# Gate of the latent attention: two heads with features on partitions, or four heads with tokens on partitions and transposes

## The chip, the cores and the metric

One core of a Trainium2 chip runs the whole program. The metric is the device time of one execution, in microseconds (us); the median of three runs of the kernel before is 2054.03 us.

The engines in this text are TensorE (PE in the profile, its weight loads are PEld), VectorE (DVE), ScalarE (ACT) and the queue that issues the loads from memory (SP). Each works through its own list of instructions in the order in which the list stands; semaphores make one engine wait for another.

## What is computed

Two layers of a network over 256 positions (tokens) of width 2048. Each layer normalises its input to `h`, multiplies it by one wide matrix `w_in`, and runs two branches; the change is in the second, the latent attention with 16 heads:

```python
proj = h @ w_in
rq, rk, rv, rg, cq, ckv, kr, mg, bg = jnp.split(proj, points, axis=-1)
q  = (rms_norm(cq, g_cq) @ w_uq)      # per head 128 + 64 (rotary) columns
kv = (rms_norm(ckv, g_ckv) @ w_ukv)   # per head 128 key and 128 value columns
o_mla = mla_attention(q_nope, q_rope, k_nope, k_rope, v)   # chunk-causal softmax
y_mla = (o_mla * jax.nn.silu(mg)) @ w_mla_proj
```

`mg` is the gate of the title: 2048 columns of `h @ w_in`, 128 for each head. All arithmetic is in fp32.

## The kernel before, in words

Matrix products run in three passes. A weight slice of 1024 values per partition is loaded into a tile `wst` (five buffers), ScalarE writes its high part into a tile `whl` (L240), VectorE the rest, the low part (L241), and TensorE multiplies high by high, high by low and low by high (L273 twice, L276 once, in `chunk`; `mm3` on L263 to L265 is the same for small operands). There are three `whl` buffers, so the split of a slice waits until the matmuls of the slice three before it are over.

`proj` gives a product with features on partitions: the weights are the stationary operand, `h` streams with 256 columns. `proj_tok` gives it with tokens on partitions: `h` is stationary, the weights stream with 512 columns, and two accumulators are filled, one for each half of the tokens. Accumulators `acc` come from four buffers in PSUM, other PSUM tiles `aux` from four more.

The attention loop (from `for g in range(MH // 2)`) does a pair of heads per turn, eight turns per layer. A turn has these steps: the query projection (36 matmuls from `cq`), whose results go to `qkn` and, through `rope_mla` (L483 to L485, VectorE), to the rotary part; the key and value projection (48 matmuls from `ckv`); the scores (L848, L849, `mm3`); the softmax (L852 to L866, on VectorE and ScalarE); the gate projection `mg` (L874, L875: 96 matmuls, then a Silu on ScalarE); the transposes of the softmax's result `sm` (L882), split into `p1` (L883) and copied to `pT` (L884); the product with the values (L888, L889) into `po`; the multiplication of `po` by the gate (L891, VectorE), and the split into `z` (L892), which `w_mla_proj` is multiplied with later.

A scheduler that knows the dependencies and the number of buffers orders each engine's list when the program is built. It mixes turns: the values product of a turn stands among the projections of the next. In the background, slices of `w_mod` for a later stage are loaded at a fixed rate per weight slice and accumulated on VectorE (L402, L367 when one is finished). Each weight slice's split has raised priority.

Of the kernel before, what the change touches and what calls it, by code (L numbers as in the profile page):

```python
# [13 lines left out]
AF = mybir.ActivationFunctionType  # L14
ALU = mybir.AluOpType
AX = mybir.AxisListType

P = 128
S = 256
# [19 lines left out]
C_MG = C_KR + ROPE  # L39
# [69 lines left out]
def trunk(ctx: ExitStack, tc: tile.TileContext, x, c, positions, w_mod, b_mod, g_norm, w_in, g_cq,  # L109
          g_ckv, w_uq, w_ukv, w_ret_proj, w_mla_proj, w_out, g_final, consts, decay, out):  # L110
    nc = tc.nc
    V, A, T, DMA = nc.vector, nc.scalar, nc.tensor, nc.sync
# [11 lines left out]
    def acc_tile():  # L124
        return pacc.tile([P, 2, S], F32, name="acc", tag="acc")

    def aux_tile():
        return paux.tile([P, 512], F32, name="aux", tag="aux")

    def tmp_tile():  # L130
        return tp.tile([P, 512], F32, name="tmp", tag="tmp")
# [4 lines left out]
    def quarter(name, dtype=F32):  # L136
        return big.tile([P, 1024], dtype, name=name, tag="quarter")
# [5 lines left out]
    def tokens(name):  # L143

        return quarter(name).rearrange("p (t f) -> p t f", t=2)
# [20 lines left out]
    ident = cst[:, K_ID : K_ID + P]  # L166
# [72 lines left out]
    def split_into(hi, lo, src):  # L239
        A.activation(hi, src, AF.Copy)  # L240
        return V.tensor_tensor(lo, src, hi.bitcast(F32), ALU.subtract)  # L241
# [7 lines left out]
    def load_split(src, nk, n, early=False):  # L249
        if prepared and not early:  # L250
            return prepared.pop(0)
        bg()
        w = load(src, nk, n)
        t = hp.tile([P, 2, 1024], F32R, name="whl", tag="whl")
        hi = t[:, 0, : nk * n].rearrange("p (k n) -> p k n", k=nk)
        lo = t[:, 1, : nk * n].rearrange("p (k n) -> p k n", k=nk)
        with tc.high_priority(offset=SPLITS):
            last_split.append(split_into(hi, lo, w))
        return hi, lo
# [7 lines left out]
    def chunk(todo):  # L267


        for o, w, a, start, _, moves in todo:  # L270
            for i in range(2):
                x, y = (a[i], w[0]) if moves else (w[0], a[i])
                T.matmul(o, x, y, start=start and i == 0, stop=False, skip_group_check=True)  # L273
        for o, w, a, _, stop, moves in todo:
            x, y = (a[0], w[1]) if moves else (w[1], a[0])
            T.matmul(o, x, y, start=False, stop=stop, skip_group_check=True)  # L276

    def proj_chunk(accs, hi, lo, k0, nk, span, act):

        chunk([(accs[j // 2][:, j % 2, :], (hi[:, k, j * P : (j + 1) * P], lo[:, k, j * P : (j + 1) * P]),  # L280
                act.block(k0 + k), k0 + k == span[0] and j % 2 == 0, k0 + k == span[1] - 1, False)
               for k in range(nk) for j in range(hi.shape[2] // P)])

    def proj(w, col, n, act, span=(0, KT)):
        accs = [acc_tile() for _ in range((n + 2 * P - 1) // (2 * P))]
        nk = 1024 // n
        for k0 in range(*span, nk):
            hi, lo = load_split(w[k0 * P : (k0 + nk) * P, col : col + n], nk, n)
            proj_chunk(accs, hi, lo, k0, nk, span, act)
        return accs  # L290

    def proj_tok(w, col, act, span=(0, KT)):

        accs = [acc_tile() for _ in range(2)]
        for k0 in range(*span, 2):
            hi, lo = load_split(w[k0 * P : (k0 + 2) * P, col : col + 512], 2, 512)
            chunk([(accs[t].rearrange("p a b -> p (a b)"), (hi[:, k, :], lo[:, k, :]),
                    act.block(k0 + k, slice(t * P, (t + 1) * P)), k0 + k == span[0], k0 + k == span[1] - 1, True)
                   for k in range(2) for t in range(2)])
        return [a.rearrange("p a b -> p (a b)") for a in accs]  # L300
# [325 lines left out]
    def layer(l, r, u):  # L626
        W = w_in[l]

        if l == 0:
            r, hh = start()  # L630
        else:
            hh = Pairs("h")
# [93 lines left out]
        for sg in range(2):  # L726
# [5 lines left out]
            for pr in range(2):  # L732
                g = 2 * sg + pr
# [6 lines left out]
                for h in range(2):  # L740
                    ps = aux_tile()
# [5 lines left out]
                    po = aux_tile()  # L747
# [42 lines left out]
        for g in range(MH // 2):  # L790
            def two(t, f0, n):
                return t[:, f0 : f0 + 2 * n].rearrange("p (a b) -> p a b", a=2)

            t1 = quarter("qkn")
            qn, kn, qr = two(t1, 0, P), two(t1, 256, P), t1[:, 512:768]
            t1 = quarter("q1", F32R)
            q1, r1 = (two(t1, 0, P), two(t1, 256, P)), (t1[:, 512:640], t1[:, 640:768])
            t1 = quarter("k1", F32R)
# [4 lines left out]
            for k0 in (0, 2):  # L803
                w = load(w_uq[l, k0 * P : (k0 + 2) * P, g * 2 * QW : (g + 1) * 2 * QW], 2, 2 * QW)
                w = w.rearrange("p k (h d) -> p k h d", h=2)
                t = hp.tile([P, 2, 1024], F32R, name="whl", tag="whl")
# [5 lines left out]
                for k in range(2):  # L812
                    kt = k0 + k
                    b = cq.block(kt)
# [10 lines left out]
            for k0 in (0, 2):  # L825
                hi, lo = load_split(w_ukv[l, k0 * P : (k0 + 2) * P, g * 512 : (g + 1) * 512], 2, 512)
                todo = []
                for k in range(2):
                    kt = k0 + k
                    b = ckv.block(kt)  # L830
# [15 lines left out]
            for h in range(2):  # L846
                ps = aux_tile()
# [17 lines left out]
                    i = 2 * t + h  # L865
                    V.tensor_scalar(sm[:, h, rng[t]], sm[:, h, rng[t]], rec[:, i : i + 1], None, ALU.mult)  # L866

            t1 = quarter("mg")
            mg, pT = two(t1, 0, S), two(t1, 512, P)
            t1 = quarter("p1", F32R)  # L870
            p1 = two(t1, 0, S), two(t1, 512, S)
            t1 = quarter("v1", F32R)
            v1 = t1[:, 0:256], t1[:, 256:512]
            accs = proj(W, C_MG + g * 256, 256, hh)  # L874
            A.activation(mg, accs[0], AF.Silu)  # L875

            split_into(*v1, vv[:, 0, :])
            po = aux_tile()
            for h in range(2):
                ps = aux_tile()  # L880
# [4 lines left out]
            for h in range(2):  # L885
# [1 line left out]
                o = po[:, h * S : (h + 1) * S]  # L887
                mm3(o, [u[:, es] for u in v1], [u[:, h, :] for u in p1], True, False)  # L888
                T.matmul(o[:, P:S], vv[:, 1, es], pT[:, h, :], start=False, stop=True, skip_group_check=True)  # L889
            zt = tmp_tile()  # L890
            V.tensor_tensor(zt, po, mg.rearrange("p a b -> p (a b)"), ALU.mult)  # L891
            split_into(*zz.flat(g), zt)  # L892


# [2 lines left out]
        for n in range(4):  # L897
# [6 lines left out]
            for a in range(2):  # L904
                ps = aux_tile()
                for b in range(2):
                    f = (2 * a + b) * P
# [9 lines left out]
        for f0, nf in ((0, 4), (4, 4), (8, 4), (12, 2), (14, 2)):  # L917
            accs = proj(w_out[l], f0 * P, nf * P, mm)
            with tc.high_priority() if f0 == 14 else nullcontext():
                for a, acc in enumerate(accs):  # L920
                    for b in range(2):
                        f = f0 + 2 * a + b
# [91 lines left out]
    for l in range(DEPTH):  # L1014
        r, u = layer(l, r, u)
# [22 lines left out]
```

## Time and profile before

| what | before |
|---|---|
| median of three runs | 2054.03 us (2052.9 to 2054.82) |
| the profiled execution, whole | 2052.09 us |
| its span | 2050.3 us |
| TensorE busy in the span | 2021.5 us, 99% |
| VectorE busy | 1483.7 us, 72% |
| ScalarE busy | 1061.3 us, 52% |
| DMA, mean | 225 GB/s |
| chain that ended last | 96% TensorE |

Busy times overlap between engines. A matmul's recorded duration is longer than the distance to the next one's start, since matmuls are pipelined; what a matmul costs is read from start to start.

### The profile page before, as it was taken

To read this page: it belongs to the slowest core of one execution; us is meant where nothing else is said; L and a number is where in the kernel's file an instruction comes from. 1 tells how busy PE (TensorE), PEld (TensorE's weight loads), DVE (VectorE), ACT (ScalarE), POOL (GpSimd) and SP (SyncE) were. 2 spreads that over 40 slices of the span, in tenths; PEclk is the share of its full clock that TensorE was granted. 3 is DMA by queue.
4 is the path that set the end of the run, shared out by engine and by line. 5 is a ranking of instruction groups with operands and counts; after the bars stand their busy time and mean duration, and the time that the engine had idled before them with its cause. 6 is when DMAs were issued, how large, how long until landed. Compare 5 with 4: busy or idle time off the path is not lost.

```text
span 2050.3 us, 31775 instructions
## 1 busy us (share of the span) xinstructions
PE 2021.5 (99%) x12412; PEld 1804.9 (88%) x12414; DVE 1483.7 (72%) x2083; ACT 1061.3 (52%) x1489; POOL 0.2 (0%) x4
## 2 busy tenths in 40 slices
PE   7999999999999999999999999999999999999998
PEld 4888898998899998889998888889889999988887
DVE  5789986778777877775577775568766877765574
ACT  4554355554466665444454463455534666644453
POOL 0000000000000000000000000000000000000000
PEclk9999999999999999999999999999999999999999
DMA  8998966567866668875569966665677666666672
GB/s 314 334 293 290 311 194 189 163 197 256 302 186 196 195 195 272 284 261 186 184 202 337 323 208 190 191 183 154 196 245 222 201 186 195 210 224 192 188 244 92
DMA packets 251222, 460.59 MB, mean 225 GB/s; under 512 B 18464, under 2 KB 68032, under 8 KB 251072
## 3 DMA queue, kind: packets, MB, share of 16 engines
q1 hardware_dynamic: 251072, 458.57, 70.2%
q8 instruction: 97, 1.59, 0.3%
q14 instruction: 53, 0.43, 0.1%
HBM read 456.41 MB, written 2.10 MB: 224 GB/s over the span
## 4 chain that ended last, share of the span: by engine, by line
PE 96%; DVE 1%; DMA 1%; ACT 1%; issue 0%; SPq 0%; ACTq 0%; DVEq 0%
PE acc L273 58%; PE acc L276 29%; DMA wmod<-in_w_mod 1%; PE aux L264 1%; PE aux L265 1%; PE aux L263 1%; PE acc L263 1%; PE acc L264 1%; PE acc L265 1%; DVE extra L349 0%; PE aux L882 0%; PE aux L723 0%; PE aux L909 0%; PE aux L848 0%; PE aux L849 0%
## 5 line engine op out<-in xcount | busy, mean ns | idle before, releaser
L240 ACT ACTIVATE whl<-wst 128x1024 fp32r<-128x1024 f32 (+1 forms) x708 | 709.1, 1007 | 809.1 <-PE acc L276 694.7
L241 DVE TENSOR_TENSOR whl<-wst,whl 128x1024 fp32r<-128x1024 f32 (+1 forms) x708 | 814.2, 1156 | 381.2 <-ACT whl L240 377.5
L273 PE MATMUL acc<-whl,h 128*128 128x512 f32 x2048 | 512.2, 391 | 0.0
L273 PEld LDWEIGHTS acc<-whl,h 128*128 128x128 f32 x2048 | 382.1, 188 | 78.3
L273 PE MATMUL acc<-h,whl 128*128 128x256 f32 x2432 | 327.2, 285 | 4.0 <-ACT h L240 2.4
L273 PEld LDWEIGHTS acc<-h,whl 128*128 128x128 f32 x2432 | 307.5, 192 | 6.2 <-ACT h L240 3.2
L276 PE MATMUL acc<-whl,h 128*128 128x512 f32 x1024 | 278.4, 391 | 0.0
L273 PE MATMUL acc<-whl,z 128*128 128x512 f32 x1024 | 254.1, 390 | 1.2 <-ACT whl L240 1.2
L273 PEld LDWEIGHTS acc<-whl,z 128*128 128x128 f32 x1024 | 191.9, 188 | 41.3 <-ACT whl L240 1.6
L276 PEld LDWEIGHTS acc<-whl,h 128*128 128x128 f32 x1024 | 191.3, 188 | 39.2 <-DVE whl L241 0.2
L276 PE MATMUL acc<-h,whl 128*128 128x256 f32 x1216 | 176.2, 284 | 0.0
L276 PEld LDWEIGHTS acc<-h,whl 128*128 128x128 f32 x1216 | 158.6, 192 | 0.0
L276 PE MATMUL acc<-whl,z 128*128 128x512 f32 x512 | 137.2, 390 | 0.0
L402 DVE SCALAR_TENSOR_TENSOR macc<-ring,cact,macc 128x1024 f32<-128x1024 f32 x75 | 96.1, 1281 | 31.5 <-DMA ring<-in_w_mod 31.4
L402 DVE SCALAR_TENSOR_TENSOR macc<-wst,cact,macc 128x1024 f32<-128x1024 f32 x90 | 115.0, 1278 | 0.0
L276 PEld LDWEIGHTS acc<-whl,z 128*128 128x128 f32 x512 | 96.0, 188 | 20.1 <-DVE whl L241 0.2
L273 PE MATMUL acc<-c,whl 128*128 128x256 f32 x640 | 101.1, 289 | 0.0
L273 PEld LDWEIGHTS acc<-c,whl 128*128 128x128 f32 x640 | 86.3, 191 | 0.3
L273 PE MATMUL acc<-m,whl 128*128 128x256 f32 x512 | 67.3, 283 | 0.0
L273 PEld LDWEIGHTS acc<-m,whl 128*128 128x128 f32 x512 | 64.0, 192 | 0.1
L276 PE MATMUL acc<-c,whl 128*128 128x256 f32 x320 | 57.9, 285 | 0.0
L273 PE MATMUL acc<-whl,m 128*128 128x512 f32 (+1 forms) x256 | 56.5, 365 | 0.0
(263 smaller groups left out, 1871.9 us busy)
## 6 DMA issues: line engine op xcount, KB each, us to landing
wst<-in_w_in SPq DMA_DIRECT2D x416, 512.0 KB, 4.5
wst<-in_w_mod SPq DMA_DIRECT2D x96, 512.0 KB, 4.7
ring<-in_w_mod SPq DMA_DIRECT2D x80, 512.0 KB, 5.4
wst<-in_w_ret_proj SPq DMA_DIRECT2D x64, 512.0 KB, 5.0
wst<-in_w_mla_proj SPq DMA_DIRECT2D x64, 512.0 KB, 4.2
wst<-in_w_out SPq DMA_DIRECT2D x64, 512.0 KB, 3.6
wst<-in_w_ukv SPq DMA_DIRECT2D x32, 512.0 KB, 4.5
wst<-in_w_uq SPq DMA_DIRECT2D x32, 384.0 KB, 4.2
```

What stands on the lines that cost most here:

```text
L240: A.activation(hi, src, AF.Copy)
L241: return V.tensor_tensor(lo, src, hi.bitcast(F32), ALU.subtract)
L263: T.matmul(o, a[0], b[0], start=start, stop=False, skip_group_check=True)
L264: T.matmul(o, a[0], b[1], start=False, stop=False, skip_group_check=True)
L265: T.matmul(o, a[1], b[0], start=False, stop=stop, skip_group_check=True)
L273: T.matmul(o, x, y, start=start and i == 0, stop=False, skip_group_check=True)
L276: T.matmul(o, x, y, start=False, stop=stop, skip_group_check=True)
L402: V.scalar_tensor_tensor(macc, w, cact[:, k : k + 1], macc, ALU.mult, ALU.add)
```

## The change

The gate projection runs only in even turns, for four heads at once, with tokens on partitions; its result `mg` is kept for two turns. In each turn the two heads' part is transposed on TensorE into a PSUM tile (L894), copied out by ScalarE (L895), and `po` is multiplied by the copy (L896). `pT` moves from the gate's tile into `qkn`'s.

```diff
-            qn, kn, qr = two(t1, 0, P), two(t1, 256, P), t1[:, 512:768]
+            qn, kn, qr, pT = two(t1, 0, P), two(t1, 256, P), t1[:, 512:768], two(t1, 768, P)
...
-            t1 = quarter("mg")
-            mg, pT = two(t1, 0, S), two(t1, 512, P)
...
-            accs = proj(W, C_MG + g * 256, 256, hh)
-            A.activation(mg, accs[0], AF.Silu)
+            if g % 2 == 0:
+                mg = tokens("mg")
+                for t, acc in enumerate(proj_tok(W, C_MG + g * 256, hh)):
+                    A.activation(mg[:, t, :], acc, AF.Silu)
...
-            zt = tmp_tile()
-            V.tensor_tensor(zt, po, mg.rearrange("p a b -> p (a b)"), ALU.mult)
+            ps, zt = aux_tile(), tmp_tile()
+            for h in range(2):
+                for t in range(2):
+                    f = g % 2 * S + h * P
+                    T.transpose(ps[:, h * S + t * P : h * S + (t + 1) * P], mg[:, t, f : f + P], ident)
+            A.activation(zt, ps, AF.Copy)
+            V.tensor_tensor(zt, po, zt, ALU.mult)
             split_into(*zz.flat(g), zt)
```

The order on each engine moves with it. First place: TensorE in layer 0, from the end of turn 2's key and value projection to the start of its gate projection; the values product of turn 1 (`p` and `v` are its operands, `qkn` or `mg` holds `pT`) stands here. Before, from that product's second half on:

```order
L889 MATMUL aux<-mg,vv 128x128 [waits Activation_49]
L263 MATMUL aux<-p_5528,v_5529 128x256
L264 MATMUL aux<-p_5528,v_5529 128x256 [waits DVE_49]
L265 MATMUL aux<-p_5528,v_5529 128x256
L889 MATMUL aux<-mg,vv 128x128 [waits Activation_49]
L276 MATMUL acc<-c,whl 128x256
L276 MATMUL acc<-whl,c 128x256 x2
L276 MATMUL acc<-c,whl 128x256 x2
```

and then 26 more matmuls of the key and value projection, and `L273 MATMUL acc<-h,whl 128x256`, the first of the gate, which waits for VectorE and ScalarE. Now, in the same place, with all 48 matmuls of that projection already behind:

```order
L882 MATMUL aux<-cst,sm 128x128
L263 MATMUL aux<-p_5558,v_5559 128x256 [waits Activation_49]
L894 MATMUL aux<-cst,mg 128x128 x4
L264 MATMUL aux<-p_5558,v_5559 128x256 [waits DVE_49]
L265 MATMUL aux<-p_5558,v_5559 128x256
L889 MATMUL aux<-qkn,vv 128x128 [waits Activation_49]
L263 MATMUL aux<-p_5558,v_5559 128x256
L264 MATMUL aux<-p_5558,v_5559 128x256 [waits DVE_49]
L265 MATMUL aux<-p_5558,v_5559 128x256
L889 MATMUL aux<-qkn,vv 128x128 [waits Activation_49]
L273 MATMUL acc<-whl,h 128x512 [waits DVE_49]
```

The six transposes of `sm`, the values product and the gate's first matmul now follow each other without projection work between them. The gate's first matmul waits for the instruction of VectorE that frees a rotary accumulator (L484), as it did before.

Second place: VectorE over the same stretch. Before, from the low part of `p1` to the rotary products of turn 2 (`tmp<-acc,sin_t`, `qkn<-acc,cos_t`):

```order
L241 TENSOR_TENSOR p_5528<-aux,p_5528 128x256 [waits Activation_49] x2
L241 TENSOR_TENSOR whl<-wst,whl 128x1024 [waits DMAHW4_49,Activation_49]
L241 TENSOR_TENSOR whl<-wst,whl 128x1024 [waits DMAHW5_49,DVE_49,Activation_49]
L891 TENSOR_TENSOR tmp<-aux,mg 128x512 [waits PE_49]
L483 TENSOR_TENSOR tmp<-acc,sin_t 32x256 x4
L484 TENSOR_TENSOR qkn<-acc,cos_t 128x256
```

Now:

```order
L241 TENSOR_TENSOR whl<-wst,whl 128x1024 [waits DMAHW6_49,Activation_49]
L402 SCALAR_TENSOR_TENSOR macc<-wst,cact,macc 128x1024 [waits DMAHW7_49]
L241 TENSOR_TENSOR whl<-wst,whl 128x1024 [waits DMAHW0_49,Activation_49]
L241 TENSOR_TENSOR p_5558<-aux,p_5558 128x256 [waits Activation_49] x2
L483 TENSOR_TENSOR tmp<-acc,sin_t 32x256 x4
L896 TENSOR_TENSOR tmp<-aux,tmp 128x512 [waits PE_49]
L484 TENSOR_TENSOR qkn<-acc,cos_t 128x256
```

The last `whl` split (the gate's third slice) and, here, a background slice moved ahead of the low part of `p1`; the rotary products stay behind it, and the gate's multiplication (L896, L891 before) now stands between L483 and L484. On ScalarE the high part of that third slice likewise stands ahead of the high part of `p1`; it writes into the `whl` buffer of turn 2's last key and value slice.

## Rows read from the trace of the kernel before

**Rows 1.** The page, parts 1 and 2: busy us; tenths in 40 slices

```profile
PE 2021.5 (99%) x12412; PEld 1804.9 (88%) x12414; DVE 1483.7 (72%) x2083; ACT 1061.3 (52%) x1489; POOL 0.2 (0%) x4
...
PE   7999999999999999999999999999999999999998
```

**Rows 2.** Busy us of each engine in one turn (windows: PE, PEld, DVE, ACT)

```profile
598.80:624.50 25.70, 25.70 (x218) 25.70 (x217) 19.28 (x38) 16.60 (x34) 0.00 (x0) 1.00 0.63 187
```

**Rows 3.** PE in order of time: start us, us, instructions; 512 columns, then 256

```profile
543.98 1.98 PE L273 MATMUL acc<-whl,z 128*128 128x512 f32 x8
545.79 1.07 PE L276 MATMUL acc<-whl,z 128*128 128x512 f32 x4
...
581.18 2.08 PE L273 MATMUL acc<-h,whl 128*128 128x256 f32 x16
583.10 1.12 PE L276 MATMUL acc<-h,whl 128*128 128x256 f32 x8
```

**Rows 4.** PE in order of time around six transposes

```profile
821.48 0.82 PE L909 MATMUL aux<-cst,tmp 128*128 128x128 f32 x6
822.05 0.94 PE L276 MATMUL acc<-whl,h 128*128 128x512 f32 x3
822.82 1.55 PE L273 MATMUL acc<-whl,h 128*128 128x512 f32 x6
```

**Rows 5.** Instructions of line 882: duration ns min/median/max, first and last start

```profile
L882 PE MATMUL aux<-cst,sm x96: 270/272/277, 588.4 to 1769.9; 128*128 128x128 f32 x96
```

**Rows 6.** PE in order of time: values product, rest of turn, gate

```profile
619.65 0.28 PE L264 MATMUL aux<-p,v 128*128 128x256 f32 x1
...
620.94 0.40 PE L276 MATMUL acc<-whl,c 128*128 128x256 f32 x2
...
624.52 2.08 PE L273 MATMUL acc<-h,whl 128*128 128x256 f32 x16
```

**Rows 7.** DVE in order of time, over the same stretch

```profile
616.67 0.75 DVE L241 TENSOR_TENSOR p<-aux,p 128x256 fp32r<-128x256 f32 x2
...
621.02 0.69 DVE L891 TENSOR_TENSOR tmp<-aux,mg 128x512 f32<-128x512 f32 x1 [0.72 <-PE aux L889]
621.74 1.72 DVE L483 TENSOR_TENSOR tmp<-acc,sin_t 32x256 f32<-32x256 f32 x4
623.47 0.42 DVE L484 TENSOR_TENSOR qkn<-acc,cos_t 128x256 f32<-128x256 f32 x1
623.81 1.22 DVE L241 TENSOR_TENSOR whl<-wst,whl 128x1024 fp32r<-128x1024 f32 x1
624.95 1.28 DVE L402 SCALAR_TENSOR_TENSOR macc<-wst,cact,macc 128x1024 f32<-128x1024 f32 x1
```

**Rows 8.** ACT in order of time, over the same stretch

```profile
613.98 1.28 ACT L875 ACT_TABLE_LOAD   x1
...
616.07 0.65 ACT L240 ACTIVATE p<-aux 128x256 fp32r<-128x256 f32 x2
616.60 1.07 ACT L240 ACTIVATE whl<-wst 128x1024 fp32r<-128x1024 f32 x1
617.55 0.45 ACT L884 ACTIVATE mg<-aux 128x128 f32<-128x128 f32 x2
```

**Rows 9.** Who waited for line 484 (us in total, times)

```profile
  PE acc L273: 0.3, 1
```

**Rows 10.** Windows where the granted clock (PEclk) is lower or PE is idle

```profile
36.00:38.00 2.00, 0.99 (x5) 1.02 (x6) 1.97 (x7) 0.19 (x1) 0.00 (x0) 0.50 1.03 383
2044.00:2046.00 2.00, 0.00 (x0) 0.00 (x0) 1.75 (x6) 1.23 (x2) 0.00 (x0) 1.00 0.00 0
```

**Rows 11.** PE in order of time after the stretch at the lower clock

```profile
39.72 3.57 PE L273 MATMUL acc<-h,whl 128*128 128x256 f32 x16 [0.87 <-ACT h L558]
43.12 1.11 PE L276 MATMUL acc<-h,whl 128*128 128x256 f32 x8
```

## Prediction, made before the changed kernel ran

> **What bounds the kernel now.** I read the page's busy times first: TensorE is busy 99% of the span and in nearly every slice 9 tenths or more [rows 1]. The view of windows then shows the stage that the change touches: one turn of the attention loop lasts 25.70 us, TensorE is busy in all 25.70, VectorE in 19.28, ScalarE in 16.60 [rows 2]. So here time is TensorE's work plus whatever TensorE has to wait; what other engines gain or lose counts only where it becomes such a wait. Wait it has almost none: the view of line 484 shows one matmul that waited 0.3 us for it, in 16 turns [rows 9]. That line is worth remembering: the first matmul of the gate needs a free accumulator, and L484 frees it. In the turn of rows 6 and 7 L484 ends at 623.89 and the gate starts at 624.52 [rows 6, 7]: 0.6 us to spare, because the rest of the key and value projection, from 620.94 on, covers 3.58 us [rows 6].
>
> **The gate's matmuls.** Before, 16 turns of 96 matmuls with 256 columns, 1536; 16 of them take 581.18 to 583.10, 0.120 us each [rows 3]: 184.3 us. After, 8 projections of 96 with 512 columns, 768; 8 take 543.98 to 545.79, 0.226 us each [rows 3]: 173.8 us. All of it is on the path: **10.5 us saved**. The weight slices are as many and as large as before, so loads, splits and background slices keep their number.
>
> **The transposes.** Four in each of 16 turns, 64. Six of them with three 512-column matmuls behind last from 821.48 to 822.82, 1.34 us, of which the matmuls take 0.68 [rows 4]: 0.11 us for one, 7.0 us in all. The other end is the recorded duration of one, 0.272 us [rows 5]: 17.4 us. I take 7.0, since the rows are pipelined runs and TensorE issues these four at a time. At the low end nothing: six groups stand where TensorE waits anyway.
>
> The Trainium skill ("TensorE: Matmul & The Clock Gate", part 4, PE-mode transpose) prices a transpose at about 275 ns in a kernel's context. The recorded duration agrees, the pace does not; by the page's price the transposes would cost an estimated 17.6 us and the sum below would be 10.6 us higher.
>
> **ScalarE and VectorE.** ScalarE gains a copy per turn and loses Silu table loads (1.28 us each [rows 8]) in odd turns; VectorE's multiplication only changes an operand from `mg` to the copy. With 9 and 6 us of slack per turn [rows 2] I cost both at nothing, except where TensorE stands and waits for them, next.
>
> **The cover that is gone.** This is the main term. A turn's gate projection, 96 matmuls, hid the softmax and freed time for the values product to spread through the next turn's projections. An odd turn has no gate. The order in front shows what the scheduler does at the end of turns 1, 3 and 5 of each layer, six times: the next turn's key and value projection is already used up while the softmax runs, and then the transposes of `sm`, the values product and the next gate's first matmul stand in a row with nothing between. (Turn 7 is followed by another stage's projection, into which its values product is mixed; even turns keep the gate as cover.) What must happen on the other engines before the gate may start, counted from the end of the key and value projection, because the gate's third slice needs the buffer that this projection frees, and its split stands first on both engines:
>
> - ScalarE, high part of the third slice: 616.60 to 617.55, 0.95 [rows 8]. The high parts of `p1` come behind it.
> - VectorE, low part of the slice: 623.81 to 624.95, 1.14 [rows 7]; at 2.09.
> - low parts of `p1`: 0.75 [rows 7]; at 2.84.
> - L483, four rotary products: 621.74 to 623.47, 1.73 [rows 7]; at 4.57.
> - L896, priced as L891: 621.02 to 621.74, 0.72 [rows 7]; at 5.29. It waits for the values product, which waits for `p1`; by then it is done.
> - L484: 0.34 to the next start [rows 7]; at 5.63. Now the gate may start.
>
> TensorE's own work in these 5.63 us: six transposes of `sm` 0.66, four of the gate 0.44, and the values product, 619.65 to 620.94 less two projection matmuls plus the first of its passes, 1.17 [rows 6]; together 2.27. So it is idle **3.4 us** at least, in three pieces (for the high part of `p1`, for its low part, for L484), none above about 3 us.
>
> More stands ahead in some of the six. In the order, a background slice (L402, 1.28 [rows 7]) is ahead of `p1` in layer 0's first and layer 1's second and third; a finishing step of the background (L367, as wide as L891, 0.72) is ahead of L896 in layer 0's second; in layer 1's first, two background products push the scores back so that half the cover is used up before the softmax starts, which I price like a slice; in layer 1's third a weight split (1.14) also stands inside the softmax's scaling. That gives 4.6, 4.1, 3.4, 4.6, 4.6 and 5.8 us: **27.1 us**. The bounds are six times 3.4, 20.4, if VectorE is always free in time, and six times 5.8, 34.8, if it is always late. Nothing is queued that TensorE could do meanwhile, and since it is the bound before and after, later stages cannot give this back. A gain here is excluded: the gate's first matmul waits for L484 by a semaphore, and VectorE works in order.
>
> **The sum.** Against the profiled execution's own 2052.1 us: minus 10.5, plus 7.0, plus 27.1, gives 2075.7. The median of the runs shown is 1.9 above that execution; I forecast 2077 us, 1.1% slower. A measurement of this kernel can tell some 0.2%, 4 us, from no change.
>
> **Rivals.**
>
> *The waits are hidden: TensorE's work alone decides.* For it: the whole stage is free of waits now, with 6 us of slack per turn on VectorE [rows 2]. Against it: slack on average is no help to an order in which TensorE has nothing left to issue; the 0.6 us to spare at L484 rested on 3.58 us of projection that now stand earlier [rows 6, 7]. Time: 2052.1 - 10.5 + 7.0 = 2048.6, a gain of 0.17%, no measurable change. If the transposes too were free, because TensorE stood idle there for other reasons, 2041.6. It would decide if VectorE reached the rotary products before the projection's end, which its list forbids, as the third slice stands ahead.
>
> *The pieces of idleness also cost the clock.* The granted clock is at its lower level (0.50, which is 1.2 GHz) in the window 36 to 38, where TensorE was busy half the time [rows 10], and the next 16 matmuls took 39.72 to 43.12, 3.40 us instead of 1.92 [rows 11]: 1.5 us lost. Around each of the six places TensorE is busy 2.3 of 5.6 us, which resembles that window. Six times 1.5 is 9 us: 2085 to 2087. Against it: at the end of the span TensorE is idle in the whole window 2044 to 2046 with the clock at 1.00 [rows 10], and no piece here is longer than 3 us, with matmuls at full width right before and after. The same page of the Trainium skill (part 1) says that idleness lets the clock fall to that level, which speaks for this rival and does not enter its price.
>
> *The change does half of what I charge it with:* p1 and the rotary products run earlier than their place suggests, because VectorE is far ahead of TensorE; the wait shrinks to the last two steps, L896 and L484, 1.1 us, and the values product's own two waits, about 1 us more. Six times 2 is 12: 2061.
>
> **How the numbers follow.** My forecast, waits of 20 to 35 us, 0.70; with the clock as well, 0.13; half the waits, 0.06; hidden waits, 0.08, of which 0.03 with the transposes hidden too; the rest, 0.03, for slower than all these. The forecast's bounds in time are 2069 to 2083, plus the 1.9 of the median, and the clock takes it to 2093; I leave out most of the hidden case and the tail, and take 2063 to 2090. Slower by over 0.2%: 0.92 less a little for mistakes in reading the order, 0.89; within 0.2%: 0.08; faster: 0.03.
>
> **What the profile after would show.** For the sum: TensorE's busy time about 3 us lower at most, and new rows among its waits, 20 to 35 us in all: L273 of the gate waiting for L484 with about 2 us six times, L264 for the low part of `p1`, L263 for ScalarE's high part, all between the two layers' turns 1 and 2, 3 and 4, 5 and 6, and none around turn 0 or 7. Matmuls of 512 columns in the gate at 0.226 us. For the clock: windows with PEclk under 1.00 behind these places. I am wrong if TensorE shows no idle time at the six places, or if a wait of another kind (a load, a buffer of `sm` or `mg`) is longer than those named.

## The result, and the profile after

The changed kernel takes **2090.9 us** (2087.15 to 2091.11 in four runs) against 2054.4 for the kernel before on the same chip: 1.0177 times, 95% interval 1.0165 to 1.0189. It is 36.5 us slower; the forecast was 2077 us, with a range of 2063 to 2090. The sign and the main mechanism were right, the time lies just above the range, and a rival that had a chance of 0.13 came on top of the forecast. The profiled execution of after is one of 2091.0 us with a span of 2089.1 (before 2052.1 and 2050.3).

The page's busy times of after, the answer to [rows 1]:

```profile
PE 2038.7 (98%) x11708; PEld 1782.3 (85%) x11710; DVE 1489.3 (71%) x2083; ACT 1052.7 (50%) x1491; POOL 0.2 (0%) x4
```

TensorE has 704 matmuls fewer and is busy 17.2 us more. That alone says that idle time isn't the whole loss: it also works slower. The two attention stages by the view of windows (us, TensorE busy, instructions, granted clock), each from its first query projection to the first product behind the attention, first before, then after:

```profile
563.02:791.98 228.96, 228.70 (x1849) 1.00 0.66 199
1563.17:1792.15 228.98, 228.98 (x1831) 1.00 0.66 199
```

```profile
565.63:811.60 245.97, 235.29 (x1497) 0.97 0.59 187
1584.10:1830.97 246.87, 236.53 (x1479) 0.97 0.59 185
```

Both stages together last 492.8 us, before 457.9: 34.9 more. Of this 20.8 is idle time (21.0 against 0.3). The rest, 14.1, is in the busy time, and there the mean clock has fallen from 1.00 to 0.97. The other 3.9 us of the 38.8 between the spans lie ahead of the two stages (2.6 and 1.3) and have nothing of the gate in them; they come at the end.

The waits of TensorE in after (us in total, times, longest), without those that before has too:

```profile
PE acc L273 <- DVE qkn L484: 8.6, 6, 1.7
PE aux L264 <- DVE p L241: 6.1, 6, 1.6
...
PE aux L263 <- ACT p L240: 3.2, 4, 0.8
...
PE aux L882 <- DVE sm L866: 2.1, 2, 1.1
...
PE acc L273 <- ACT qkn L838: 0.8, 1, 0.8
...
PE aux L889 <- ACT qkn L884: 0.3, 1, 0.3
```

Of these 21.1 us, 17.9 are the waits that the prediction named (for the high part of `p1`, for its low part, for L484); two for the softmax add 2.1, one for the copy of `pT` 0.3, and one for the copy of the keys 0.8. All but the 0.8 (turn 7 of layer 0) stand between turns 1 and 2, 3 and 4, 5 and 6. TensorE in order of time at the first of the six places, from the transposes of `sm` into the gate of turn 2 (the answer to [rows 6]); the last column is the idle time ahead and who ended it:

```profile
624.77 0.60 PE L882 MATMUL aux<-cst,sm 128*128 128x128 f32 x4
626.18 0.39 PE L263 MATMUL aux<-p,v 128*128 128x256 f32 x1 [0.81 <-ACT p L240]
626.41 0.60 PE L894 MATMUL aux<-cst,mg 128*128 128x128 f32 x4
628.53 0.39 PE L264 MATMUL aux<-p,v 128*128 128x256 f32 x1 [1.52 <-DVE p L241]
...
629.84 0.63 PE L889 MATMUL aux<-qkn,vv 128*128 128x128 f32 x2
631.67 2.08 PE L273 MATMUL acc<-whl,h 128*128 128x512 f32 x4 [1.20 <-DVE qkn L484]
633.54 1.06 PE L276 MATMUL acc<-whl,h 128*128 128x512 f32 x2
...
636.51 1.09 PE L273 MATMUL acc<-whl,h 128*128 128x512 f32 x4
```

Three pieces of idle time, as forecast. But the gate that follows begins slowly: its first four matmuls take 631.67 to 633.54, 0.47 us each, and only from 636.51 on are they back at 0.23. VectorE over the same stretch, the answer to [rows 7]:

```profile
625.73 1.28 DVE L402 SCALAR_TENSOR_TENSOR macc<-wst,cact,macc 128x1024 f32<-128x1024 f32 x1
626.92 1.22 DVE L241 TENSOR_TENSOR whl<-wst,whl 128x1024 fp32r<-128x1024 f32 x1
628.06 0.75 DVE L241 TENSOR_TENSOR p<-aux,p 128x256 fp32r<-128x256 f32 x2
628.84 1.72 DVE L483 TENSOR_TENSOR tmp<-acc,sin_t 32x256 f32<-32x256 f32 x4
630.59 0.69 DVE L896 TENSOR_TENSOR tmp<-aux,tmp 128x512 f32<-128x512 f32 x1
631.20 0.42 DVE L484 TENSOR_TENSOR qkn<-acc,cos_t 128x256 f32<-128x256 f32 x1
```

This is the chain of the forecast, instruction by instruction and without a gap: background slice, third slice, `p1`, rotary products, the gate's multiplication, L484. The granted clock around the place, in windows of 4 us, and (last row) at the third place, where the same waits stand:

```profile
625.63:629.63 4.00, 1.92 (x12) 0.94 0.63 188
629.63:633.63 4.00, 2.80 (x9) 0.50 0.60 207
633.63:637.63 4.00, 4.00 (x14) 0.71 0.02 4
637.63:641.63 4.00, 4.00 (x29) 1.00 0.00 0
745.63:749.63 4.00, 2.28 (x10) 1.00 0.47 156
```

The clock goes to its lower level (0.50, 1.2 GHz) while TensorE has short work between waits, stays there into the gate, and returns. This is so at four of the six places. At the third of layer 0 and the first of layer 1 it stays at 1.00.

### The profile page after: what moved, and what is told of

It reads as the page before. It is cut to its first block, busy times and chain, and to the rows that moved or that the text cites. A ratio compares the mean times of both kernels' runs of the same rounds, so it can differ in the third digit from the quotient of the medians.

```text
span 2089.1 us, 30366 instructions
## 1 busy us (share of the span) xinstructions
PE 2038.7 (98%) x11708; PEld 1782.3 (85%) x11710; DVE 1489.3 (71%) x2083; ACT 1052.7 (50%) x1491; POOL 0.2 (0%) x4
## 4 chain that ended last, share of the span: by engine, by line
PE 91%; DVE 3%; DMA 2%; ACT 2%; issue 1%; SPq 0%; ACTq 0%; DVEq 0%
PE acc L273 56%; PE acc L276 28%; DMA wmod<-in_w_mod 1%; DMA ring<-in_w_mod 1%; DVE whl L241 1%; PE aux L264 1%; ACT whl L240 1%; PE aux L265 1%; PE aux L263 1%; PE acc L263 1%; PE acc L264 1%; PE acc L265 1%; DVE extra L349 0%; DVE macc L402 0%; DVE tmp L483 0%
## 5 line engine op out<-in xcount | busy, mean ns | idle before, releaser
L273 PE MATMUL acc<-whl,h 128*128 128x512 f32 x2560 | 649.4, 394 | 9.4 <-DVE qkn L484 8.6
L273 PEld LDWEIGHTS acc<-whl,h 128*128 128x128 f32 x2560 | 480.7, 189 | 109.9 <-DVE qkn L484 10.1
L276 PE MATMUL acc<-whl,h 128*128 128x512 f32 x1280 | 353.7, 393 | 0.5 <-DVE whl L241 0.3
L276 PEld LDWEIGHTS acc<-whl,h 128*128 128x128 f32 x1280 | 240.0, 189 | 50.5 <-DVE whl L241 1.6
L273 PE MATMUL acc<-whl,z 128*128 128x512 f32 x1024 | 254.1, 390 | 1.2 <-ACT whl L240 1.2
L273 PEld LDWEIGHTS acc<-whl,z 128*128 128x128 f32 x1024 | 191.9, 188 | 41.3 <-ACT whl L240 1.6
L273 PE MATMUL acc<-h,whl 128*128 128x256 f32 x1408 | 190.7, 287 | 3.7 <-ACT h L240 2.4
L273 PEld LDWEIGHTS acc<-h,whl 128*128 128x128 f32 x1408 | 179.5, 194 | 5.7 <-ACT h L240 3.2
L276 PE MATMUL acc<-h,whl 128*128 128x256 f32 x704 | 100.9, 286 | 0.0
L273 PE MATMUL acc<-c,whl 128*128 128x256 f32 x640 | 96.9, 284 | 0.0
L276 PEld LDWEIGHTS acc<-h,whl 128*128 128x128 f32 x704 | 92.5, 195 | 0.0
L273 PEld LDWEIGHTS acc<-c,whl 128*128 128x128 f32 x640 | 85.7, 192 | 0.6
L273 PE MATMUL acc<-m,whl 128*128 128x256 f32 x512 | 67.3, 283 | 0.0
L273 PEld LDWEIGHTS acc<-m,whl 128*128 128x128 f32 x512 | 64.0, 192 | 0.1
L276 PE MATMUL acc<-c,whl 128*128 128x256 f32 x320 | 57.1, 284 | 0.0
L273 PE MATMUL acc<-whl,m 128*128 128x512 f32 (+1 forms) x256 | 56.5, 365 | 0.0
```

## How the experiments are read

All experiments are read by the same four numbers, for both attention stages of the profiled execution together: their length; TensorE's idle time in them; what the clock took (busy time times one minus the granted clock, summed over windows of 4 us); and the rest, which is TensorE's work at full clock.

| kernel | median us | stages | idle | clock | work |
|---|---|---|---|---|---|
| before | 2054.4 | 457.9 | 0.3 | 0.0 | 457.7 |
| after | 2090.9 | 492.8 | 21.0 | 10.9 | 460.9 |
| after_again | 2092.4 | 493.0 | 21.7 | 10.0 | 461.2 |
| e1_features_four | 2116.5 | 519.6 | 33.6 | 23.0 | 463.0 |
| e2_tokens_two | 2059.2 | 464.4 | 0.0 | 0.0 | 464.4 |
| e3_no_transposes | 2104.6 | 508.0 | 34.5 | 19.7 | 453.8 |
| e6_fill | 2084.9 | 489.8 | 15.3 | 1.7 | 472.8 |
| e8_rope_copy | 2094.4 | 494.9 | 26.1 | 7.5 | 461.4 |
| e9_queries_ahead | 2063.7 | 464.0 | 8.6 | 0.0 | 455.4 |
| f2_queries_prio | 2062.4 | 461.6 | 6.9 | 0.0 | 454.6 |
| g1_half_gate | 2061.6 | 466.2 | 7.4 | 1.4 | 457.4 |
| h1_half_ahead | 2079.4 | 478.0 | 16.5 | 7.8 | 453.6 |

The ratios behind each median are to the kernel before on the same chip. The four numbers come from one execution each, and medians also carry what happens ahead of the two stages (see the sum, below), so kernels a few us apart are compared by their stages.

Theory A is that of the prediction: an odd turn without a gate leaves TensorE nothing to do at six places; with what after showed, the idle pieces also cost the clock. Theory B is that the layout with tokens on partitions, its transposes and copies cost the time.

## Four heads without transposes, two heads with them, four heads with no transposes at all

The change has two halves, four heads at a time and tokens on partitions. The first experiment does the first half alone:

```diff
-                mg = tokens("mg")
-                for t, acc in enumerate(proj_tok(W, C_MG + g * 256, hh)):
-                    A.activation(mg[:, t, :], acc, AF.Silu)
+                mg = quarter("mg")
+                for a, acc in enumerate(proj(W, C_MG + g * 256, 512, hh)):
+                    A.activation(mg[:, a * 512 : (a + 1) * 512], acc.rearrange("p a b -> p (a b)"), AF.Silu)
...
+            V.tensor_tensor(zt, po, mg[:, g % 2 * 512 : (g % 2 + 1) * 512], ALU.mult)
```

> The gate for four heads in even turns, as in the change, but with features on partitions as before the change, so with no transposes and 1536 matmuls of 256 columns. Theory A, the cover that an odd turn loses: the same six places stay, so the time stays near the changed kernel's 2091: plus 10.5 for the narrower matmuls, minus about 4.4 for the 40 transposes that do not stand in idle time there, so 2097, between 2088 and 2102, with the first gate matmul of turns 2, 4 and 6 waiting for L484 and the clock falling at some of these places. Theory B, the layout with tokens on partitions and its transposes cost the time: 2052 to 2060.

Measured: 2116.5 us (1.0299, 1.0284 to 1.0315), above the range of both theories. Theory B is out as the main cause: no transposes, and the time is higher still. But 2116 isn't 2097 either. The list of waits tells why:

```profile
PE aux L848 <- ACT qkn L838: 13.6, 6, 2.3
PE aux L264 <- DVE p L241: 9.3, 6, 2.2
```

The scheduler put the next turn's first score (L848) ahead of the gate here, and that waits 2.3 us each time for ScalarE's copy of the keys, longer than the gate waited for L484. So its 12.6 us of additional idle and 12.1 of additional clock belong to an order that after doesn't have.

The second half alone, two heads in every turn, with tokens on partitions:

```diff
-            if g % 2 == 0:
-                mg = tokens("mg")
-                for t, acc in enumerate(proj_tok(W, C_MG + g * 256, hh)):
-                    A.activation(mg[:, t, :], acc, AF.Silu)
+            mg = two(quarter("mg"), 0, S)
+            accs = [acc_tile().rearrange("p a b -> p (a b)")[:, :S] for _ in range(2)]
+            for k0 in range(0, KT, 4):
+                hi, lo = load_split(W[k0 * P : (k0 + 4) * P, C_MG + g * 256 : C_MG + (g + 1) * 256], 4, 256)
...
-                    f = g % 2 * S + h * P
+                    f = h * P
```

> The gate with tokens on partitions and transposes, as in the change, but for two heads in every turn (96 matmuls of 256 columns each), so each turn keeps its gate as cover. Theory A: no waits at the six places; 2054.4 plus 64 transposes at 0.11, 2061, between 2055 and 2063. Theory B: the transposes and their copies cost the time, 2080 or more.

Measured: 2059.2 us (1.0030, 1.0020 to 1.0041). The stages show no idle time and a clock of 1.00:

```profile
563.13:795.05 231.92, 231.92 (x1881) 1.00 0.64 197
1566.48:1798.99 232.51, 232.51 (x1863) 1.00 0.64 196
```

Work grows by 464.4 - 457.7 = 6.7 us for 64 transposes: 0.105 us for one, against the 0.11 of the prediction. ScalarE's copies add no wait, and neither does the new place of `pT`, which this kernel has too. With the cover of a gate in every turn, none of the six waits exists.

The third kernel is after without its transposes and their copy; `po` is multiplied by the gate as it lies, not by its transpose, and the rest of the work is the same:

```diff
-            ps, zt = aux_tile(), tmp_tile()
-            for h in range(2):
...
-                    T.transpose(ps[:, h * S + t * P : h * S + (t + 1) * P], mg[:, t, f : f + P], ident)
-            A.activation(zt, ps, AF.Copy)
-            V.tensor_tensor(zt, po, zt, ALU.mult)
+            zt = tmp_tile()
+            V.tensor_tensor(two(zt, 0, S), two(po, 0, S), mg[:, :, g % 2 * S : (g % 2 + 1) * S], ALU.mult)
```

> The changed kernel without the 64 transposes and without ScalarE's copies; the product is multiplied by the gate as it stands, so that part of the computation is changed. Theory A: the six places stay; 40 of 64 transposes are on the path, so 4.4 less than 2091: 2086.5, between 2083 and 2091. Theory B: 2054 to 2060.

Measured: 2104.6 us, 14 more than with the transposes; both expectations miss. Its list has the same row for L848 as e1, 13.6 us in six waits, so the order changed with the edit, and the difference to after is no price of transposes. Its work, 453.8, is 7.1 less than after's.

## Only the order changed

If the lost cover is the cause, the same operations in a better order should be nearly as fast as before. Here the next turn's query projection, with its rotary products, is written ahead of the values product; nothing else is touched.

```diff
-        for g in range(MH // 2):
...
+        def queries(g):
...
+            return qn, kn, qr, pT, q1, r1
+
+        ahead = queries(0)
+        for g in range(MH // 2):
+            qn, kn, qr, pT, q1, r1 = ahead
...
+            if g < MH // 2 - 1:
+                ahead = queries(g + 1)
             split_into(*v1, vv[:, 0, :])
```

> The changed kernel with the same operations in another order: the next turn's query projection and its rotary products are written ahead of the values product in the program. In the order of the lists the rotary products of turn 2 then end before the gate's third slice is split, and the gate's first three slices stand ahead of the values product and between its parts. Theory A: L484 is early, the gate covers the splits of p1, the six waits go and the clock with them: 2054.4 - 10.5 + 7.0 = 2051, between 2046 and 2056, granted clock 0.996 or more. Theory B (layout and transposes): stays at 2085 or more. Theory C, the waits move to another buffer or engine: 2060 to 2075.

Measured: 2063.7 us (1.0049, 1.0037 to 1.0062), 27 us less than after. TensorE at the first place, from the key and value projection's end on:

```profile
624.62 1.09 PE L273 MATMUL acc<-whl,h 128*128 128x512 f32 x4
625.55 0.62 PE L276 MATMUL acc<-whl,h 128*128 128x512 f32 x2
...
628.67 1.17 PE L273 MATMUL acc<-whl,h 128*128 128x512 f32 x4 [1.14 <-DVE q L241]
...
631.52 0.49 PE L888 MATMUL aux<-cst,sm 128*128 128x128 f32 x3
631.76 2.10 PE L273 MATMUL acc<-whl,h 128*128 128x512 f32 x8
```

The gate now starts without a wait (L484 began at 623.40), the transposes of `sm` (L888 here) stand inside it, and the waits for `p1` are gone. The clock is 1.00 in both stages, though one wait of 1.1 to 1.2 us at most places and one of 2.0 are left: a single short wait between full rows of matmuls doesn't cost the clock in this kernel. Order alone gave back 27 of 36 us, so what theory A names, the waits and the clock that they cost, is the cause of that much. The time isn't the 2051 that I expected; it lies in theory C's range, with 8.6 us of idle time that went to other places: a weight slice on ScalarE (3.5), the gate's second accumulator, freed by the split of the queries (2.3), ScalarE's copy of the values (2.0), and L484 once (0.7).

The next edit, in `queries`, gives those evacuations the raised priority of the weight splits:

```diff
-            A.activation(qn, a1[:, :, 0:P], AF.Copy)
-            split_into(*q1, a1[:, :, P:S])
-            rope_mla(qr, a2[:, 0, :])
+            with tc.high_priority(offset=SPLITS):
+                A.activation(qn, a1[:, :, 0:P], AF.Copy)
+                split_into(*q1, a1[:, :, P:S])
+                rope_mla(qr, a2[:, 0, :])
```

> The kernel e9_queries_ahead, with the evacuation of the next turn's query accumulators put ahead of other work on ScalarE and VectorE. In e9_queries_ahead six waits of about 1.2 us were left, where the gate's second accumulator waits for that evacuation behind the exponentials, or for a weight slice. Theory A: about half of these 8.6 us go: 2060, between 2056 and 2063. Theory B, the evacuation is not what they wait for: 2062 to 2067.

Measured: 2062.4 us (1.0042, 1.0027 to 1.0057), idle 6.9 instead of 8.6. It went in the expected direction, by too little to tell from e9. The two waits for the split of the queries (2.3 us) are gone, as meant, but those for L484 grew from 0.7 to 2.1.

## What the idle pieces cost apart from their length

Here TensorE is given nine useless matmuls at each of the six places, in the time in which it waits (FILL_A is 4, FILL_B 5):

```diff
             ps, zt = aux_tile(), tmp_tile()
+            if g in (1, 3, 5):
+                for _ in range(FILL_A):
+                    T.matmul(ps, p1[0][:, 0, 0:P], hh.flat(0)[0], start=True, stop=True, skip_group_check=True)
...
+            if g in (1, 3, 5):
+                fill = aux_tile()
+                for _ in range(FILL_B):
+                    T.matmul(fill, p1[1][:, 1, 0:P], hh.flat(0)[0], start=True, stop=True, skip_group_check=True)
```

> The changed kernel with nine matmuls of 512 columns more at each of the six places, whose results nobody reads: four between the first and second pass of the values product, where TensorE waits for the low part of p1 (6.1 us in all six places), five behind the product, where it waits for L484 (8.6 us). They take 9 x 0.226 x 6, 12.2 us, inside 14.7 us of idle time. Theory A, the idle pieces cost their own length and, apart from that, the clock (10.9 us in the attention stages at the lower level): the clock stays at 1.00 there and the time falls by 10.9, less up to 4 for filling that overlaps badly: 2080 to 2085, mean clock 0.996 or more. Theory B, the clock falls for another reason, or the fill only pushes the rest back: 2088 to 2100.

Measured: 2084.9 us (1.0154, 1.0140 to 1.0168; after 1.0177, 1.0165 to 1.0189). The first place in the same windows of 4 us:

```profile
625.24:629.24 4.00, 2.87 (x17) 1.00 0.65 186
629.24:633.24 4.00, 2.88 (x14) 1.00 0.65 209
633.24:637.24 4.00, 4.00 (x25) 1.00 0.01 4
```

The clock took 1.7 us instead of 10.9, in the slowest of the four executions (2087.9; the others took 2082.4 to 2085.6): TensorE is kept busy, and the clock stays up at five of six places. The fill is 11.9 us of additional work against only 5.7 us less idle time, so it gives 6.2 of the 9.2 back. That the idle pieces cost the clock, about 9 us of its 10.9, is shown by the clock itself; the total alone, whose interval overlaps that of after, wouldn't show it.

The changed kernel was profiled once more, unedited:

> The changed kernel once more, profiled, to see which of its six places lose the clock. In its first profile it was four of six. If order and idleness fix it, the same four, 10.9 us in the attention stages; if the idleness only allows it and something else in time decides, another set of places with the same waits (20 to 22 us), and a time that differs by about 2.7 us for each place more or less.

Measured: 2092.4 us, idle 21.7, clock 10.0. The same four places lose the clock and the same two keep it. In these two executions it is the same places, but not in every one is it as much: over the whole program the mean granted clock was 0.989 and 0.991 in the two, and 0.993 in the shortest of after's four (2087.2 us), which was not profiled. What tells the two places from the four stays open: the third place of layer 0 has waits of 0.81, 0.50 and 1.72 us and keeps the clock, the second has 0.76, 0.52, 0.35 and 1.68 and loses it. The two that keep it are also the shortest from the projection's end to the gate's start, 6.10 and 6.75 us against 6.79 to 7.94, too close to call that the reason.

## Taking away one wait

L484 ends the last wait of each place. With a copy by ScalarE the accumulator is free earlier:

```diff
-            rope_mla(qr, a2[:, 0, :])
+            t2 = tmp_tile()[:, :S]
+            A.activation(t2, a2[:, 0, :], AF.Copy)
+            rope_mla(qr, t2)
```

> The changed kernel with one ScalarE copy more per turn: the rotary accumulator is copied out and L483 and L484 read the copy, so the accumulator is free as soon as ScalarE has copied it. In the order of the lists the gate's first two slices then stand between the two halves of the values product. Theory A, L484 ends the last wait of each of the six places, and the waits for p1 stand apart from it: its 8.6 us and six restarts of about 0.27 go, 2081, and down to 2072 if the clock falls less often. Theory B, another condition of the gate (its third slice, an accumulator of the query projection) comes last anyway: 2088 to 2093.

Measured: 2094.4 us (1.0202, 1.0186 to 1.0216), from 2090.9, the profiled execution, to 2099.3. Theory B: the wait for L484 is gone, and in its place stands the score that waits for ScalarE's keys, as in e1:

```profile
PE aux L850 <- ACT qkn L840: 13.6, 6, 2.3
```

TensorE's order put that score ahead of the gate, so taking away the gate's last wait alone gained nothing; what the six waits for L484 cost by themselves isn't shown by it.

## A version that beats both was not found

The gate for four heads can also keep its cover if half of it stays in the odd turn:

```diff
...
+            elif g % 2 == 0:
+                mg = half
+                for t, acc in enumerate(proj_tok(W, C_MG + g * 256, hh, (KT // 2, KT))):
+                    V.tensor_tensor(mg[:, t, :], mg[:, t, :], acc, ALU.add)
+                    A.activation(mg[:, t, :], mg[:, t, :], AF.Silu)
+            elif g < MH // 2 - 1:
+                half = tokens("mg")
+                for t, acc in enumerate(proj_tok(W, C_MG + (g + 1) * 256, hh, (0, KT // 2))):
+                    A.activation(half[:, t, :], acc, AF.Copy)
```

> The gate for four heads with tokens on partitions, as in the change, but spread over two turns: an odd turn computes the first half of the sum (1024 of 2048 rows) for the next four heads and stores it, the next even turn the second half and adds. Each turn keeps 10.9 us of gate as cover (turn 0 has a whole gate, turn 7 none). Theory A, the lost cover alone makes the change slower: no waits, 2054.1 - 10.5 + 6.7 = 2050.3, between 2047 and 2054. Theory B, four heads at once or the transposes cost more, or the additional copies and additions make VectorE or ScalarE late: 2056 or more.

Measured: 2061.6 us (1.0041, 1.0028 to 1.0053). The six places have cover again, 7.4 us of idle time instead of 21.0, but not before's 0.3: L484 is still late four times, 4.3 us. Theory B has this remainder, and whether the additional steps on VectorE or the order make it is open. The clock took 1.4 us, behind one of these waits, which has full rows of matmuls on both sides:

```profile
1667.06 1.24 PE L273 MATMUL acc<-whl,h 128*128 128x512 f32 x4 [2.25 <-DVE qkn L484]
```

```profile
1665.55:1669.55 4.00, 2.49 (x10) 0.81 0.73 218
1669.55:1673.55 4.00, 4.00 (x15) 0.76 0.08 31
```

So a single wait can cost the clock too. It needn't: f2 has one of 2.24 us and a clock of 1.00 throughout.

The last kernel joins this edit with the two on the queries:

> Both cures at once: the gate for four heads spread over two turns (g1_half_gate) and the next turn's query projection ahead of the values product with its evacuation in front (f2_queries_prio). In g1_half_gate 4.3 us of waits for L484 and 2.3 for a score were left, in f2_queries_prio 6.9 us of waits in all. If each cure takes the other's waits, TensorE's work alone is left: 2054 - 10.5 + 6.7 = 2050, and with a few waits left 2050 to 2055. If the additional copies and additions are what makes the other engines late: 2058 to 2062.

Measured: 2079.4 us (1.0126, 1.0110 to 1.0143), far from both. The two cures hinder each other; its longest waits are new ones:

```profile
PE acc L273 <- ACT mg L889: 7.2, 4, 2.6
...
PE acc L273 <- ACT qkn L817: 3.6, 1, 3.6
PE acc L273 <- DVE qkn L484: 3.5, 1, 3.5
```

Gate and queries are both ahead now, and TensorE waits for ScalarE to empty an accumulator of the one (L889) or the other (L817) before it can go on. By the forecast's 10.5 for the matmuls and the measured 6.7 for the transposes, this gate without a single wait would win 3.8 us, 0.2%; that is an estimate.

## Why the prediction was right and wrong, by its steps

**The matmuls.** 10.5 us saved: not measured by itself, but e9's work fits it, 457.7 - 10.5 + 6.7 = 453.9 against 455.4 with seven breaks left in it. In after, 12 matmuls of the gate at full clock take 747.46 to 750.31, 0.238 us each with the start behind a wait; forecast 0.226.

**The transposes.** 7.0 forecast, 6.7 measured (e2). The Trainium skill ("TensorE: Matmul & The Clock Gate", part 4, PE-mode transpose) prices one at about 275 ns, an estimated 17.6 us for 64. The recorded duration agrees (0.272 in after too), but it is not what they cost; e2's difference decides that.

**The cover.** This was the main term, and it holds place by place. From the end of the key and value projection to the gate's start, less the 2.27 us of TensorE's own work: forecast 4.6, 4.1, 3.4 and 4.6, 4.6, 5.8, together 27.1; measured 4.9, 4.5, 3.8 and 4.5, 5.0, 5.7, together 28.4. The gate's starts, behind projections that end at 624.55, 682.74, 741.36, 1644.33, 1700.12 and 1758.25:

```profile
631.67 2.08 PE L273 MATMUL acc<-whl,h 128*128 128x512 f32 x4 [1.20 <-DVE qkn L484]
...
689.53 2.07 PE L273 MATMUL acc<-whl,h 128*128 128x512 f32 x4 [1.68 <-DVE qkn L484]
...
747.46 1.20 PE L273 MATMUL acc<-whl,h 128*128 128x512 f32 x4 [1.72 <-DVE qkn L484]
...
1651.08 1.21 PE L273 MATMUL acc<-whl,h 128*128 128x512 f32 x4 [1.74 <-DVE qkn L484]
...
1707.43 2.07 PE L273 MATMUL acc<-whl,h 128*128 128x512 f32 x4 [1.11 <-DVE qkn L484]
...
1766.19 2.07 PE L273 MATMUL acc<-whl,h 128*128 128x512 f32 x4 [1.11 <-DVE qkn L484]
```

The listed waits at these places sum to 20.2 us, less than 28.4, because each is counted only from the modelled end of the matmul ahead, which lies later than its share of a full row. The work fits that: after's 460.9 against 453.9 is 7 us in some 20 breaks, and e1, which has the same matmuls as before, has 463.0 against 457.7, 5.3 us in 22: by this estimate 0.2 to 0.35 for each break. The chain, counted from start to start, had this in it. The prediction's list said "about 2 us six times" for L484; it is 8.6 in six, 1.4 each.

**The clock: the step that failed.** The sum held the clock at 1.00 at the six places, a term of nothing, and the range cut the case in which it falls. The prediction had the rival and its price: six times 1.5, 2085 to 2087. It gave it 0.13, on two grounds. The first, that no piece is longer than 3 us, with matmuls at full width on both sides, is true (the longest is 1.74) and didn't matter. The second, the window 2044 to 2046 with TensorE idle and the clock at 1.00 [rows 10], was read one window short. TensorE's last matmul there ends at 2041.8, and right behind the window the clock falls:

```profile
2044.00:2046.00 2.00, 0.00 (x0) 0.00 (x0) 1.75 (x6) 1.23 (x2) 0.00 (x0) 1.00 0.00 0
2046.00:2048.00 2.00, 0.00 (x0) 0.00 (x0) 0.00 (x0) 0.00 (x0) 0.00 (x0) 0.60 0.94 383
```

So it shows a fall that comes late, not one that stays away. The row that did resemble the place, half busy and the clock at 0.50 [rows 10, 11], was in the prediction and was overruled. In after the first twelve matmuls of the gate, 2.71 us at 0.226, take 4.84, 4.92, 2.85, 2.89, 4.59 and 4.24: 8.1 us more in all; with what lies ahead of the gate the clock took 10.9. That the rival's 9 us came near to this is luck: it was to be six places at 1.5, and it was four at about 2.7.

Where TensorE idles in short pieces, the Trainium skill ("TensorE: Matmul & The Clock Gate", part 1, A second HAM failure mode: psum-queue depth-cycling) describes a kernel in which TensorE idles briefly between groups of matmuls, so often that its clock goes back and forth. The rows of after agree (pieces of 0.35 to 1.68 us at the places that lose it), and that sentence speaks for the rival. By the Trainium skill ("TensorE: Matmul & The Clock Gate", part 4, PE-mode transpose) a transpose does not count as busy in the same way. The runs can say this much: e1 and e3, without the gate's transposes, lose more to the clock than after (23.0 and 19.7), so it falls without those; the six of `sm` stayed in every run and weren't tried.

**The sum.** In the stages: -10.5 + 6.7 + 28.4 + 8.1 = 32.7 of 34.9; the wait of 0.8 in turn 7 is a part of the rest, 1.4 stays unassigned. Outside them, 3.9 us: the start of the program at the lower clock ([rows 10, 11] in after lasts until 45.09, 1.0 longer), a place at 122 us that shows how thin the line is (about 1.5), and 1.3 between the two stages, at a clock of 1.00, of unknown cause. First before, then after:

```profile
121.27 0.50 PE L273 MATMUL acc<-h,whl 128*128 128x256 f32 x2 [1.45 <-ACT h L240]
```

```profile
122.39 0.50 PE L273 MATMUL acc<-h,whl 128*128 128x256 f32 x2 [1.45 <-ACT h L240]
```

The work and the wait are the same. Behind it the window 124 to 128 has a clock of 1.00 before and 0.58 after. None of the kernels edits what stands ahead of the first attention stage, and all twelve profiles have this wait of 1.45. In four (before, e2, e8, g1) the clock stays at 1.00 behind it, and the stage begins between 563.0 and 563.6; in eight it falls, and the stage begins between 565.2 and 566.2. So some 2 us of a difference between two profiles here can be this place and have nothing of the gate in them. What decides it stays open.

Against the sum's own 2075.7 the profiled 2091.0 is 15.3 more: 8.1 for the clock, 3.9 outside the stages, 1.3 more cover, 0.8 and 1.4, less 0.3 for the transposes, 15.2 in all.

**The other rivals** are out: the waits are not hidden (2048.6), nor half of them (2061). The statement on busy time, at most 3 us lower, was wrong: it is 17.2 higher. In the stages it is 14.1 higher, of which 10.9 are the clock, since a slow matmul counts as busy for longer, and 3.2 are work: 7 in the breaks above, less the 3.8 that matmuls and transposes save.

**The range** ended at 2090 although the text took the clock's case up to 2093: with 0.13 that case was small enough to cut.

## What to carry to other kernels

When work is batched over two iterations, ask what it covered in the iteration that loses it: here fewer, wider matmuls were to save 10.5 us (e9 fits that), and the lost cover cost 28.4. Price such a place by the in-order chain of the other engines from start to start, not by the idle time that a list of waits will show, and give the clock a term wherever several short pieces of idle time come together: here it took about 2.7 us at each place that lost it, more than the 1.5 that the row at the start of the program had given. Before taking the batching back, try the order: writing the next iteration's first step ahead of this one's last gave back 27 of 36 us.

## What the runs showed of the hardware

- The granted clock fell from 1.00 to 0.50 at places of after where no piece of idle time was longer than 1.68 us, three or four pieces with 2.3 us of work among them in 6.8 to 7.9 us. Single waits of 1.1 to 2.0 us between full rows of matmuls (e9) left it at 1.00; single waits of about 2.2 us went either way (0.76 to 0.81 around one of 2.25 in g1, 1.00 with one of 2.24 in f2).
- It fell at the same four of six places in two executions of the same kernel, and yet at 122 us the same wait of 1.45 us was followed by 1.00 in four profiles and by a lower clock in eight.
- Useless matmuls in the idle time keep the clock up (e6: 1.7 us lost instead of 10.9).
- A break in a row of matmuls costs more than the idle time printed for it, by an estimate 0.2 to 0.35 us (e1 against before, after against the sum of its terms).
